# TensorE's order in a loop over pairs of experts: from a scheduler's to one written in the source, staggered over three pairs

## The chip, the cores and the metric

The kernel runs on one core of one Trainium2 chip. The metric is the device time of one execution in microseconds (us). A core has five engines that run side by side, each through its own list of instructions in order: TensorE (PE in the profile: matrix products and transposes), VectorE (DVE), ScalarE (ACT), GpSimd (POOL) and SyncE (SP, which here issues the loads of weights). PE writes its results into PSUM banks, and DVE and ACT empty them.

## What is computed

A transformer of two layers, 512 tokens by 1024 features, all float32. Layer 0 mixes tokens by differential attention, layer 1 by compressed and selected sparse attention; behind each stands a mixture of experts. All projections are modulated by vectors that come from a condition (adaLN). The change is in the experts alone:

```python
MOE_GROUPS = 4; MOE_EXPERTS_PER_GROUP = 8      # 32 experts
MOE_TOP_K = 2; MOE_HIDDEN = D_MODEL // 4       # two experts a token, hidden 256
...
# per token and chosen expert e:
#   h = silu(x @ w_gate[e]) * (x @ w_up[e]);  out += weight * (h @ w_down[e])
```

## The kernel before

The 32 experts are taken as 16 pairs (`NPAIR`). Each expert has 64 slots for its tokens, so a pair has 128 rows. `experts` (L892 to L914) loops over the pairs; for each it queues loads of weights (`w.fetch`, on SP), gathers the 128 token rows by an indirect DMA on POOL (`gather`, L826), and calls `pair` (L830 to L890). One pair is worked in these steps, whose letters are used from here on:

- **R**: 8 transposes of the gathered rows `xg` (L840) into two PSUM banks of the kind `b_tr`, four in each; each of the 8 results is modulated on its way to `xT`, by DVE (L847) and ACT (L845) in turn.
- **G**: the products with gate and up (L852), 16 for each of the two experts, in one bank `b_mm`. The two experts' instructions use 64 of the array's columns each and run side by side; PE counts 32 instructions. Behind them ACT makes `sl` (L855) and DVE multiplies it to `ac` (L857).
- **H**: 2 transposes of `ac` (L861) into a bank `b_tr`, copied to `aTm` by `copy_any`, which takes ACT (L382) and DVE (L383) in turn, call by call: for one pair the one, for the next the other.
- **D**: the product with down, 16 instructions (L875), 8 into a bank `b_sc` (the first 512 features, z = 0), 8 into a `b_mm` (z = 1). DVE scales each half to `y` (L878), ACT rounds it to `yh` (L358), DVE makes the rest `yl` (L359).
- **A**: the rows are added to their tokens. DVE builds a 0/1 matrix `st` (L869); for each of 4 blocks of tokens and 2 halves z, two products (L886 with `yh`, L887 with `yl`) of 128 columns give a bank, `b_sc` for z = 0, `b_mm` for z = 1, and DVE adds it to the accumulator `xs` (L888). That is 16 instructions on PE and 8 additions on DVE.

PSUM has two banks `b_tr`, two `b_sc` and four `b_mm`; a bank is written again only when its readers are through. Weights lie in buffers that are freed by their last use: a pair's 12 pieces of 512 KB are 6.29 MB.

In the source, pair q runs R, G, H, then A of pair q-1 (`between`), then D. The order that each engine gets is set by a scheduler when the program is built; it moves instructions among pairs as it sees fit. `overflow` calls `pair` too, for experts with more than 64 tokens; its branch is not taken with these inputs.

```python
aT = mp.tile([P, 2, P], F32, name="aTm", bufs=2)
copy_any(aT.rearrange("p k t -> p (k t)"), b[:, 0:HID])
if between is not None:
    between()
```

Of the kernel before, what the change touches and what calls it, by code (L numbers as in the profile page):

```python
# [11 lines left out]
F32 = mybir.dt.float32  # L12
# [69 lines left out]
def tile_kernel(ctx, tc, x, c, positions, ada_w, ada_b, norm_g, final_g, diff_w_in, diff_w_out,  # L82
# [3 lines left out]
    nc = tc.nc  # L86
    mm = nc.tensor.matmul
    x_d = x.rearrange("b s d -> (b s) d")
# [296 lines left out]
    class Experts:  # L385
# [65 lines left out]
    def x_first():  # L451
        for t in range(NT):
            nc.sync.dma_start(o_n[:, t, :], x_d[t * P:(t + 1) * P, :])
            normed(m, o_n[:, t, :], o_n[:, t, :], r0[:, t:t + 1], ("a", 2))
        for k in range(KC):
            b = bank("tr")
            for t in range(NT):
                nc.tensor.transpose(b[:, t * P:(t + 1) * P], by_k(o_n[:, t, :])[:, k, :], ident)
            copy_any(xT[k // 4][:, k % 4, :], b)
# [23 lines left out]
    def qk_unit(u, before=None):  # L483
# [34 lines left out]
    def diff_rows(h, i, qs, kh, kl, v, hc):  # L518
# [15 lines left out]
        for j in range(i + 1):  # L534
            nc.tensor.transpose(b[:, j * P:(j + 1) * P], a[:, j * P:(j + 1) * P], ident)
        aT = m.tile([P, 512], F32, name="aT", bufs=2)
# [77 lines left out]
    def o_trans(h):  # L614
        b = bank("tr")
        for i in range(NT):
            nc.tensor.transpose(b[:, i * P:(i + 1) * P], o_n[:, i, h * P:(h + 1) * P], ident)
        stack_k(b, o_hi[:, h, :], o_lo[:, h, :])
# [63 lines left out]
    def logits(g, lb, t):  # L682

        xk = by_k(g.xs[:, t, :])
        for q in range(2):
            b = bank("tr")
            for kk in range(4):
                nc.tensor.transpose(b[:, kk * P:(kk + 1) * P], xk[:, 4 * q + kk, :], ident)
            ht = g.mp.tile([P, 512], F32, name="ht", tag="xT", bufs=2)
# [139 lines left out]

    def pair(g, q, tab, gu, dn, xg, between=None):  # L830


        mp = g.mq
        toks, tokf, wts = tab
        xT = g.mp.tile([P, KC, P], F32, name="xT", bufs=2)
        for z in range(2):
            b = bank("tr")
            for kk in range(4):
                k = 4 * z + kk
                nc.tensor.transpose(b[:, kk * P:(kk + 1) * P], by_k(xg)[:, k, :], ident)  # L840
            for kk in range(4):
# [4 lines left out]
                else:  # L846
                    nc.vector.tensor_scalar(xT[:, k, :], src, g.Ac[:, k:k + 1], g.shc[:, k:k + 1],  # L847
                                            op0=OP.mult, op1=OP.add)
        hb = bank("mm")
        for k in range(KC):  # L850
            for a in range(2):
                mm(hb[64 * a:64 * a + 64, :].rearrange("p (z n) -> p z n", z=2), xT[:, k, 64 * a:64 * a + 64], gu(a, k),  # L852
                   start=(k == 0), stop=(k == KC - 1), skip_group_check=True)
        sl = mp.tile([P, HID], F32, name="sl", bufs=2)
        nc.scalar.activation(sl, hb[:, 0:HID], AF.Silu)  # L855
        ac = mp.tile([P, HID], F32, name="ac", bufs=2)
        nc.vector.tensor_tensor(ac.rearrange("p (k t) -> p t k", k=2), hb[:, HID:512].rearrange("p (t k) -> p t k", k=2),  # L857
                                sl.rearrange("p (t k) -> p t k", k=2), op=OP.mult)
        b = bank("tr")
        for k in range(2):  # L860
            nc.tensor.transpose(b[:, k * P:(k + 1) * P], ac[:, k * P:(k + 1) * P], ident)  # L861
        aT = mp.tile([P, 2, P], F32, name="aTm", bufs=2)
        copy_any(aT.rearrange("p k t -> p (k t)"), b[:, 0:HID])
        if between is not None:
            between()
        yh = mp.tile([P, D], F32R, name="yh", bufs=1)
# [13 lines left out]

        def add():
            for t in range(NT):
                for z in range(2):
                    zz = slice(z * 512, (z + 1) * 512)
                    b = bank("mm" if z else "sc")
                    mm(b, st[:, t * P:(t + 1) * P], yh[:, zz], start=True, stop=False)  # L886
                    mm(b, st[:, t * P:(t + 1) * P], yl[:, zz], start=False, stop=True)  # L887
                    nc.vector.tensor_tensor(g.xs[:, t, zz], g.xs[:, t, zz], b, op=OP.add)  # L888

        return add  # L890

    def experts(l, g, w, later):  # L892
# [11 lines left out]
        overflow(l, g, g.xg[-1])  # L904
        add = None
        for q in range(NPAIR):
            e = 2 * q
            w.fetch(q=q, paced=DEPTH_X)
            if q:
                gather(tab, q, g.xg[q % len(g.xg)])  # L910
            add = pair(g, q, tab,
                       lambda a, k: w.gu(e + a, k), lambda a, k, z: w.dn(e + a, k, z), g.xg[q % len(g.xg)], add)
        add()
        g.st2.close()  # L914

    def overflow(l, g, xg):
# [20 lines left out]
        with tc.If(cv > STEP):  # L937
            base = g.mq.tile([P, 1], F32, name="base")
            nc.vector.memset(base, 0.0)
            with tc.For_i(1, OVER, 1):  # L940
# [3 lines left out]
                for q in range(NPAIR):  # L944
                    gather(tab, q, xg)
                    pair(g, q, tab, gu(q), dn(q), xg)()

# [23 lines left out]
    def h_k(k):  # L971
        b = bank("tr")
        for t in range(NT):
            nc.tensor.transpose(b[:, t * P:(t + 1) * P], by_k(xr[t // 2][:, t % 2, :])[:, k, :], ident)
        modulate(qp, ("wh", 4), b, k, Ac, shc, hi, lo)
# [20 lines left out]
    def evac_cs(t, acc):  # L996
# [7 lines left out]
        for s in range(4):  # L1004
            nc.tensor.transpose(b[:, s * P:(s + 1) * P], tmp[:, 2 * s:2 * s + 2, :].rearrange("p a d -> p (a d)"), ident)
        bv = b.rearrange("p (s t) -> p s t", s=4)
# [6 lines left out]
        for s in range(2):  # L1013
            nc.tensor.transpose(b[:, s * P:(s + 1) * P], tmp[:, 8 + 2 * s:10 + 2 * s, :].rearrange("p a d -> p (a d)"),
                                ident)
# [3 lines left out]
    def evac_wg(t, acc):  # L1019
# [10 lines left out]
        for s in range(2):  # L1030
            nc.tensor.transpose(b[:, s * P:(s + 1) * P], tmp[:, 2 * s:2 * s + 2, :].rearrange("p a d -> p (a d)"), ident)
        for gi in range(2):
            stack_k(b[:, gi * P:(gi + 1) * P], kst["w"][gi][0][:, tt], kst["w"][gi][1][:, tt])

    def q_unit(gi):
# [6 lines left out]
        def evac(t, acc):  # L1042
# [4 lines left out]
            for half in range(2):  # L1047
                b = bank("tr")
                for s in range(4):
                    c0 = 2 * (half * 4 + s)  # L1050
                    nc.tensor.transpose(b[:, s * P:(s + 1) * P], tmp[:, c0:c0 + 2, :].rearrange("p a d -> p (a d)"),
                                        ident)
# [12 lines left out]
    b = bank("tr")  # L1065
    nc.tensor.transpose(b[:, 0:32], pos32, ident[0:32, 0:32])
    posT = m.tile([P, 32], F32, name="posT")
# [43 lines left out]
    for k in range(2):  # L1111
        nc.tensor.transpose(b[:, k * P:(k + 1) * P], hc[:, k * P:(k + 1) * P], ident)
    hcT = m.tile([P, 2, P], F32, name="hcT", tag="pcT", bufs=2)
# [24 lines left out]
    def nsa_block(gi, i):  # L1138
# [5 lines left out]
        for zi, nm in ((1, "s"), (2, "w")):  # L1144
            if nm == "w":
# [132 lines left out]
```

## Time and profile before

| | us |
|---|---|
| median of 3 runs | 1421.07 (1418.88 to 1423.15) |
| the profiled execution | 1417.2 |
| its span in the trace | 1415.4 |
| PE busy in the span | 1289.2 (91%) |
| DVE busy | 787.2 (56%) |
| ACT busy | 513.0 (36%) |
| POOL busy | 188.4 (13%) |

The span is the time from the first to the last recorded instruction; the profiled execution's own time is 1.8 us longer. The two loops over experts lie at 399 to 681 us (layer 0) and 1122.6 to 1404.4 us (layer 1). A busy time counts an instruction from its start to its end, waits left out.

### The profile page before, as it was taken

How to read it: one execution, taken by the hardware profiler on the slowest of the kernel's cores; microseconds unless marked ns; L12 is line 12 of the kernel's file. 1: busy time of each engine (PE TensorE's matmuls, PEld its weight loads, DVE VectorE, ACT ScalarE, POOL GpSimd, SP SyncE). 2: the span in 40 equal slices, each digit the busy share in tenths (PEclk: the TensorE clock that was granted, in tenths of full speed). 3: DMA queues.
4: the chain of work that ended last, by engine and by line, in shares of the span. 5: the costliest groups of instructions: out<-in, count | busy, mean ns of one | idle time of the engine just before them, and what ended most of it. 6: DMA issues, size and time to landing. Idle time of an engine off the chain costs nothing.

```text
span 1415.4 us, 18254 instructions
## 1 busy us (share of the span) xinstructions
PE 1289.2 (91%) x6431; PEld 760.4 (54%) x6431; DVE 787.2 (56%) x1791; ACT 513.0 (36%) x1188; POOL 188.4 (13%) x298
## 2 busy tenths in 40 slices
PE   4899999978879999999799799999999599999995
PEld 0687658567733544444588465556558434444342
DVE  2444756486535666655653365657635445666555
ACT  2453544454322222111453345555644222222212
POOL 0022020211110000000042211112120200000000
PEclk7999999989979999999899999999999799999998
DMA  8633673585569999992132474520063599999931
GB/s 265 218 92 129 226 236 122 185 280 194 181 240 362 389 408 407 380 346 95 52 110 90 126 251 138 139 70 1 30 183 119 167 363 376 401 409 408 363 144 60
DMA packets 104494, 309.82 MB, mean 219 GB/s; under 512 B 13776, under 2 KB 27568, under 8 KB 104388
## 3 DMA queue, kind: packets, MB, share of 16 engines
q1 hardware_dynamic: 93920, 288.59, 57.4%
q0 software_dynamic: 6240, 12.95, 2.7%
q10 hardware_dynamic: 4228, 6.96, 1.6%
q8 instruction: 55, 0.90, 0.3%
q14 instruction: 51, 0.42, 0.1%
HBM read 310.51 MB, written 6.33 MB: 224 GB/s over the span
## 4 chain that ended last, share of the span: by engine, by line
PE 65%; DVE 6%; DMA 3%; ACT 2%; issue 1%; POOL 1%; DVEq 0%; POOLq 0%; ACTq 0%
PE b_mm L852 17%; PE b_mm L1202 5%; PE b_sc L875 4%; PE b_mm L875 4%; PE b_tr L1197 3%; PE b_sc L886 2%; PE b_tr L840 2%; PE b_mm L886 2%; DVE xs L888 2%; PE b_mm L350 2%; PE b_mm L572 2%; PE b_mm L573 2%; PE b_mm L351 2%; PE b_mm L352 2%; PE b_mm L574 2%; PE b_sc L887 2%
## 5 line engine op out<-in xcount | busy, mean ns | idle before, releaser
L852 PE MATMUL b_mm<-slot,xT 128*64 128x512 f32 x640 | 200.0, 607 | 0.0
L852 PE MATMUL b_mm<-ring,xT 128*64 128x512 f32 x384 | 135.9, 597 | 0.0
L350 PE MATMUL b_mm<-wh,h_hi 128*128 128x512 f32 (+1 forms) x320 | 116.6, 394 | 8.3 <-ACT wh L346 6.6
L351 PE MATMUL b_mm<-wl,h_hi 128*128 128x512 f32 (+1 forms) x320 | 122.1, 390 | 0.0
L352 PE MATMUL b_mm<-wh,h_lo 128*128 128x512 f32 (+1 forms) x320 | 119.9, 386 | 0.0
L845 ACT ACTIVATE xT<-b_tr,col_sh,col_A 128x128 f32<-128x128 f32 x128 | 56.4, 454 | 148.2 <-DVE xT L847 146.9
L852 PEld LDWEIGHTS b_mm<-slot,xT 128*64 128x64 f32 x640 | 58.3, 139 | 87.7 <-issue 81.7
L888 DVE TENSOR_TENSOR xs<-xs,b_sc 128x512 f32<-128x512 f32 x128 | 83.1, 680 | 23.1 <-PE b_sc L887 23.1
L888 DVE TENSOR_TENSOR xs<-xs,b_mm 128x512 f32<-128x512 f32 x128 | 81.9, 679 | 19.3 <-PE b_mm L887 19.3
L826 POOL DMA_INDIRECT xg<-xr_d,toks x32 | 32.1, 1003 | 434.1 <-PE b_tr L840 417.5
L189 PE MATMUL b_mm<-ring,csil 128*32 128x512 f32 x384 | 79.2, 645 | 10.5 <-DMA ring<-in_ada_w_dram 5.6
L855 ACT ACTIVATE sl<-b_mm 128x256 f32<-128x256 f32 x32 | 12.3, 384 | 187.7 <-PE b_mm L852 187.7
L857 DVE TENSOR_TENSOR ac<-b_mm,sl 128x256 f32<-128x256 f32 x32 | 19.8, 618 | 108.4 <-ACT sl L855 108.4
L347 DVE TENSOR_TENSOR wl<-ring,wh 128x512 fp32r<-128x512 f32 (+1 forms) x80 | 53.6, 679 | 38.3 <-ACT wh L346 37.6
L374 DVE TENSOR_REDUCE nm<-b_sc 128x1 f32<-128x128 f32 (+3 forms) x116 | 54.4, 482 | 32.2 <-PE b_sc L369 31.2
L350 PEld LDWEIGHTS b_mm<-wh,h_hi 128*128 128x128 f32 x320 | 60.5, 192 | 20.1 <-ACT wh L346 7.5
L1199 ACT ACTIVATE pT<-b_tr 128x512 f32<-128x512 f32 x80 | 47.3, 597 | 62.6 <-PE b_tr L1197 62.2
L358 ACT ACTIVATE yh<-y 128x512 fp32r<-128x512 f32 x64 | 39.9, 632 | 79.4 <-DVE y L878 79.4
L352 PEld LDWEIGHTS b_mm<-wh,h_lo 128*128 128x128 f32 x320 | 60.7, 190 | 11.0
L351 PEld LDWEIGHTS b_mm<-wl,h_hi 128*128 128x128 f32 x320 | 60.6, 190 | 10.9
L852 PEld LDWEIGHTS b_mm<-ring,xT 128*64 128x64 f32 x384 | 39.9, 137 | 49.4 <-issue 46.7
L346 ACT ACTIVATE wh<-ring 128x512 fp32r<-128x512 f32 (+1 forms) x80 | 48.4, 614 | 46.3 <-PE b_mm L352 38.0
(327 smaller groups left out, 2683.5 us busy)
## 6 DMA issues: line engine op xcount, KB each, us to landing
ring<-in_ada_w_dram SPq DMA_DIRECT2D x96, 512.0 KB
slot<-in_moe_w_gate_dram SPq DMA_DIRECT2D x80, 512.0 KB
slot<-in_moe_w_up_dram SPq DMA_DIRECT2D x80, 512.0 KB
dn<-in_moe_w_down_dram SPq DMA_DIRECT2D x80, 512.0 KB
slot<-in_moe_w_down_dram SPq DMA_DIRECT2D x48, 512.0 KB
ring<-in_moe_w_gate_dram SPq DMA_DIRECT2D x48, 512.0 KB
ring<-in_moe_w_up_dram SPq DMA_DIRECT2D x48, 512.0 KB
ring<-in_diff_w_in_dram SPq DMA_DIRECT2D x24, 512.0 KB
```

The source lines that it names most:

```text
L189: mm(acc[32 * g:32 * g + 32, :], lhsT, w[:, c0:c0 + 512], start=(k == 0), stop=(k == KC - 1), skip_group_check=True)
L347: nc.vector.tensor_tensor(wl[:, :n], w[:, k, :], wh[:, :n].bitcast(F32), op=OP.subtract)
L350: mm(accs[t][:, :n], hi[:, k, tt], wh[:, :n], start=(k == 0), stop=False)
L351: mm(accs[t][:, :n], hi[:, k, tt], wl[:, :n], start=False, stop=False)
L352: mm(accs[t][:, :n], lo[:, k, tt], wh[:, :n], start=False, stop=(k == KC - 1))
L374: nc.vector.tensor_reduce(nm, b[:, :n], axis=AX.X, op=OP.max, negate=True)
L845: nc.scalar.activation(xT[:, k, :], src, AF.Identity, scale=g.Ac[:, k:k + 1], bias=g.shc[:, k:k + 1])
L852: mm(hb[64 * a:64 * a + 64, :].rearrange("p (z n) -> p z n", z=2), xT[:, k, 64 * a:64 * a + 64], gu(a, k), start=(k == 0), stop=(k == KC - ...
L875: mm(yb[64 * a:64 * a + 64, :], aT[:, k, 64 * a:64 * a + 64], dn(a, k, z), start=(k == 0), stop=(k == 1), skip_group_check=True)
L886: mm(b, st[:, t * P:(t + 1) * P], yh[:, zz], start=True, stop=False)
L888: nc.vector.tensor_tensor(g.xs[:, t, zz], g.xs[:, t, zz], b, op=OP.add)
L1202: mm(ob[64 * st:64 * st + 64, :], vst[nm][:, j, 64 * gi:64 * gi + 64], pTs[st], start=(nm == "s" and j == 0), stop=False, skip_group_check ...
```

## The change

`mm` and `transpose` become helpers that, while the name "PE" is in a set, tell the scheduler to keep the instruction where the source has it. The set holds "PE" from the first to the last instruction of the loop over pairs, and nowhere else. `pair` is split into `rows_in` (R), `gate_up` (G), `by_hidden` (H) and `down` (D, which hands back its 8 additions), and the loop works on three pairs at a time: G of pair q+1, with additions of pair q-1 in it by twos (four products each) behind k = 1, 3, 5 and 7, H of pair q, R of pair q+2, D of pair q. A wider limit for the loads goes with it.

```diff
+    def pin(i, engine):
+        return tc.keep_in_program_order(i) if engine in pinned else i
+    def mm(*a, **k):
+        return pin(nc.tensor.matmul(*a, **k), "PE")
...
-                if e >= 2 * q + (N_GU if kind == "g" else N_DN):
+                if e >= (2 * q + N_GU if kind == "g" else 2 * max(q - 1, 0) + N_DN):
...
-            e = 2 * q
-            w.fetch(q=q, paced=DEPTH_X)
-            if q:
-                gather(tab, q, g.xg[q % len(g.xg)])
-            add = pair(g, q, tab,
-                       lambda a, k: w.gu(e + a, k), lambda a, k, z: w.dn(e + a, k, z), g.xg[q % len(g.xg)], add)
-        add()
+            nxt = None
+            if q + 2 < NPAIR:
+                gather(tab, q + 2, g.xg[q % 2])
+            w.fetch(q=q + 1, paced=DEPTH_X)
+            if q + 1 < NPAIR:
+                nxt = gate_up(g, xT, gus(q + 1), some)
+            aT = by_hidden(g, ac)
+            while adds:
+                adds.pop(0)()
+            if q + 2 < NPAIR:
+                xT = rows_in(g, g.xg[q % 2])
+            adds = down(g, q, tab, aT, lambda a, k, z: w.dn(2 * q + a, k, z))
+            ac = nxt
+        for a in adds:
+            a()
```

Ahead of the loop stand R and G of pair 0 and R of pair 1. At the end, G of pair 15 holds the additions of pair 13; then come H and D of pair 14, H of pair 15, the additions of pair 14, D of pair 15 and its additions. Every engine has as many instructions of each kind as before, POOL in the same order; outside the two loops PE's order is the same.

On PE before, around one of the last pairs of layer 0 (`ring` and `slot` are weights of gate and up, `dn` of down):

```order
L852 MATMUL b_mm<-ring_72,xT 64x512
L852 MATMUL b_mm<-ring_73,xT 64x512
L861 MATMUL b_tr<-ident,ac 128x128 x2
L840 MATMUL b_tr<-ident,xg_3359 128x128 x4
L875 MATMUL b_sc<-dn_7732,aTm 64x512
L875 MATMUL b_sc<-dn_7735,aTm 64x512
```

H stands right behind the G whose `ac` it takes, and four transposes of the next pair stand between it and D. The same engine after the change, a steady pair of layer 0:

```order
L94 MATMUL b_mm<-slot_6425,xT 64x512
L94 MATMUL b_mm<-slot_6507,xT 64x512
L94 MATMUL b_sc<-yh,st 128x512
L94 MATMUL b_sc<-yl,st 128x512
L94 MATMUL b_mm<-yh,st 128x512
L94 MATMUL b_mm<-yl,st 128x512
L97 MATMUL b_tr<-ident,ac 128x128 x2
L97 MATMUL b_tr<-ident,xg_3358 128x128 x8
L94 MATMUL b_sc<-dn_3571,aTm 64x512
L94 MATMUL b_sc<-dn_3574,aTm 64x512
```

The last two additions stand between G and H, H takes the `ac` of the pair before G's, and all eight transposes R of a later pair stand between H and D. (All of PE's lines there are L94 or L97, the helpers.)

On DVE before, a pair in the middle of layer 0 whose `aTm` DVE copies:

```order
L878 SCALAR_TENSOR_TENSOR y<-b_sc,tw,bc 128x512
L878 SCALAR_TENSOR_TENSOR y<-b_mm,tw,bc 128x512
L359 TENSOR_TENSOR yl<-y,yh 128x512 x2
L857 TENSOR_TENSOR ac<-b_mm,sl 128x128x2
L888 TENSOR_TENSOR xs<-xs,b_sc 128x512 x2
L888 TENSOR_TENSOR xs<-xs,b_mm 128x512 x3
L383 COPY aTm<-b_tr 128x256
```

And after, a steady pair whose `aTm` DVE copies (every second one; in the others ACT has the copy, and DVE's list is the same without it):

```order
L872 TENSOR_TENSOR ac<-b_mm,sl 128x128x2
L908 TENSOR_TENSOR xs<-xs,b_sc 128x512
L908 TENSOR_TENSOR xs<-xs,b_mm 128x512
L891 TENSOR_SCALAR st<-iota_t,tv 128x512
L394 COPY aTm<-b_tr 128x256
L855 TENSOR_SCALAR xT<-b_tr,col_A_2994,col_sh_2992 128x128 x4
L900 SCALAR_TENSOR_TENSOR y<-b_sc,tw,bc 128x512
L370 TENSOR_TENSOR yl<-y,yh 128x512
L900 SCALAR_TENSOR_TENSOR y<-b_mm,tw,bc 128x512
L370 TENSOR_TENSOR yl<-y,yh 128x512
```

The copy of `aTm` stands behind `ac` of the next pair, two additions and `st`; the four `xT` of a later pair stand behind it, and then `y` and `yl`, half by half.

## Rows read from the trace of the kernel before

**Rows 1.** Windows by stage of both loops; columns in the first line

```profile
core 0: us, PE busy (x) PEld busy (x) DVE busy (x) ACT busy (x) POOL busy (x), PEclk, DMA share, GB/s
409.61:577.16 167.55, 162.78 (x741) 75.36 (x741) 100.40 (x183) 35.76 (x76) 9.90 (x10) 0.99 1.01 390
577.16:667.96 90.80, 86.11 (x371) 37.21 (x369) 51.92 (x94) 17.59 (x37) 2.97 (x3) 1.00 0.74 271
667.96:681.00 13.04, 8.49 (x34) 4.03 (x34) 8.68 (x15) 3.55 (x6) 0.04 (x1) 0.98 0.07 27
...
1133.17:1300.70 167.53, 162.76 (x740) 75.36 (x741) 100.41 (x183) 35.75 (x76) 9.88 (x10) 0.99 1.00 390
1300.70:1391.49 90.79, 86.10 (x371) 37.23 (x369) 51.93 (x94) 17.59 (x37) 2.97 (x3) 1.00 0.63 237
1391.49:1404.40 12.91, 8.49 (x34) 4.03 (x34) 8.67 (x15) 3.42 (x6) 0.00 (x0) 0.99 0.00 0
```

**Rows 2.** Chain of work, layer 0, first pairs: start, length, engine, tile, line

```profile
418.69 0.86 PE b_mm L852 x4
419.55 0.66 PE b_sc L886 x2
420.21 0.47 PE b_sc L887 x2
420.68 1.01 PE b_mm L852 x4
...
427.05 0.54 DVE ac L857
427.59 2.30 DVE xs L888 x4
429.89 0.40 DVE st L869
430.29 0.34 DVE aTm L383
```

**Rows 3.** Chain of work, a pair in the middle of layer 0

```profile
471.35 5.15 PE b_mm L852 x24
...
479.02 0.22 PE b_tr L861 x2
...
479.71 0.45 PE b_tr L840 x4
...
481.54 1.87 PE b_mm L875 x8
483.40 1.72 PE b_mm L852 x8
```

**Rows 4.** PE's instructions in time order, waits ahead of them in brackets

```profile
430.68 3.02 PE L875 MATMUL b_sc<-dn,aTm 128*64 128x512 f32 x8 [2.05 <-DVE aTm L383]
...
593.00 0.59 PE L852 MATMUL b_mm<-ring,xT 128*64 128x512 f32 x1
...
595.99 0.44 PE L861 MATMUL b_tr<-ident,ac 128*128 128x128 f32 x2 [1.11 <-DVE ac L857]
```

**Rows 5.** DVE and ACT in time order, `sl` and `aTm` of one pair

```profile
476.57 0.39 ACT L855 ACTIVATE sl<-b_mm 128x256 f32<-128x256 f32 x1 [3.07 <-PE b_mm L852]
479.28 0.38 ACT L382 ACTIVATE aTm<-b_tr 128x256 f32<-128x256 f32 x1 [2.33 <-PE b_tr L861]
```

**Rows 6.** DVE in time order, from `y` to `yl` of one pair

```profile
413.69 0.75 DVE L878 SCALAR_TENSOR_TENSOR y<-b_sc,tw,bc 128x512 f32<-128x512 f32 x1 [0.65 <-PE b_sc L875]
...
417.23 0.69 DVE L359 TENSOR_TENSOR yl<-y,yh 128x512 fp32r<-128x512 f32 x1 [0.38 <-ACT yh L358]
```

**Rows 7.** DVE in time order, the end of layer 0's loop

```profile
678.34 2.47 DVE L888 TENSOR_TENSOR xs<-xs,b_mm 128x512 f32<-128x512 f32 x4
```

**Rows 8.** Windows of ten and twenty us inside the loop, columns as in rows 1

```profile
430.00:440.00 10.00, 9.32 (x36) 3.02 (x36) 4.88 (x10) 2.98 (x6) 0.99 (x1) 0.83 0.84 299
500.00:520.00 20.00, 20.00 (x98) 9.09 (x96) 11.74 (x22) 5.22 (x12) 1.91 (x2) 1.00 1.03 407
```

More of the change, by code (lines that the diff above doesn't have):

```diff
@@ L86, in tile_kernel, with transpose @@
     nc = tc.nc
-    mm = nc.tensor.matmul
+    pinned = set()
+    def pin(i, engine):
+        return tc.keep_in_program_order(i) if engine in pinned else i
+    def mm(*a, **k):
+        return pin(nc.tensor.matmul(*a, **k), "PE")
+    def transpose(*a):
+        return pin(nc.tensor.transpose(*a), "PE")
     x_d = x.rearrange("b s d -> (b s) d")
@@ L457, in x_first @@
             for t in range(NT):
-                nc.tensor.transpose(b[:, t * P:(t + 1) * P], by_k(o_n[:, t, :])[:, k, :], ident)
+                transpose(b[:, t * P:(t + 1) * P], by_k(o_n[:, t, :])[:, k, :], ident)
             copy_any(xT[k // 4][:, k % 4, :], b)
@@ L499, in evac @@
                     c0 = 2 * (half * 4 + s)
-                    nc.tensor.transpose(b[:, s * P:(s + 1) * P], tmp[:, c0:c0 + 2, :].rearrange("p a d -> p (a d)"),
+                    transpose(b[:, s * P:(s + 1) * P], tmp[:, c0:c0 + 2, :].rearrange("p a d -> p (a d)"),
                                         ident)
@@ L534, in diff_rows @@
         for j in range(i + 1):
-            nc.tensor.transpose(b[:, j * P:(j + 1) * P], a[:, j * P:(j + 1) * P], ident)
+            transpose(b[:, j * P:(j + 1) * P], a[:, j * P:(j + 1) * P], ident)
         aT = m.tile([P, 512], F32, name="aT", bufs=2)
@@ L616, in o_trans @@
         for i in range(NT):
-            nc.tensor.transpose(b[:, i * P:(i + 1) * P], o_n[:, i, h * P:(h + 1) * P], ident)
+            transpose(b[:, i * P:(i + 1) * P], o_n[:, i, h * P:(h + 1) * P], ident)
         stack_k(b, o_hi[:, h, :], o_lo[:, h, :])
@@ L687, in logits @@
             for kk in range(4):
-                nc.tensor.transpose(b[:, kk * P:(kk + 1) * P], xk[:, 4 * q + kk, :], ident)
+                transpose(b[:, kk * P:(kk + 1) * P], xk[:, 4 * q + kk, :], ident)
             ht = g.mp.tile([P, 512], F32, name="ht", tag="xT", bufs=2)
@@ L828, in gather, with rows_in @@
                                      bounds_check=S - 1, oob_is_err=False)
-    def pair(g, q, tab, gu, dn, xg, between=None):
-        mp = g.mq
-        toks, tokf, wts = tab
+    def rows_in(g, xg):
         xT = g.mp.tile([P, KC, P], F32, name="xT", bufs=2)
@@ L839, in pair @@
                 k = 4 * z + kk
-                nc.tensor.transpose(b[:, kk * P:(kk + 1) * P], by_k(xg)[:, k, :], ident)
+                transpose(b[:, kk * P:(kk + 1) * P], by_k(xg)[:, k, :], ident)
             for kk in range(4):
@@ L848, in pair, with gate_up @@
                                             op0=OP.mult, op1=OP.add)
+        return xT
+    def gate_up(g, xT, gu, between=None):
+        mp = g.mq
         hb = bank("mm")
@@ L853, in pair @@
                    start=(k == 0), stop=(k == KC - 1), skip_group_check=True)
+            if between is not None:
+                between(k)
         sl = mp.tile([P, HID], F32, name="sl", bufs=2)
@@ L858, in pair, with by_hidden, down @@
                                 sl.rearrange("p (t k) -> p t k", k=2), op=OP.mult)
+        return ac
+    def by_hidden(g, ac):
         b = bank("tr")
         for k in range(2):
-            nc.tensor.transpose(b[:, k * P:(k + 1) * P], ac[:, k * P:(k + 1) * P], ident)
-        aT = mp.tile([P, 2, P], F32, name="aTm", bufs=2)
+            transpose(b[:, k * P:(k + 1) * P], ac[:, k * P:(k + 1) * P], ident)
+        aT = g.mq.tile([P, 2, P], F32, name="aTm", bufs=2)
         copy_any(aT.rearrange("p k t -> p (k t)"), b[:, 0:HID])
-        if between is not None:
-            between()
+        return aT
+    def down(g, q, tab, aT, dn):
+        mp = g.mq
+        toks, tokf, wts = tab
         yh = mp.tile([P, D], F32R, name="yh", bufs=1)
@@ L879, in pair, with add @@
             stack_k(y, yh[:, zz], yl[:, zz])
[L881 to L890, printed above, removed]
+        def add(t, z):
+            zz = slice(z * 512, (z + 1) * 512)
+            b = bank("mm" if z else "sc")
+            mm(b, st[:, t * P:(t + 1) * P], yh[:, zz], start=True, stop=False)
+            mm(b, st[:, t * P:(t + 1) * P], yl[:, zz], start=False, stop=True)
+            nc.vector.tensor_tensor(g.xs[:, t, zz], g.xs[:, t, zz], b, op=OP.add)
+        return [lambda t=t, z=z: add(t, z) for t in range(NT) for z in range(2)]
     def experts(l, g, w, later):
@@ L904, in experts, with gus, some @@
         overflow(l, g, g.xg[-1])
-        add = None
-        for q in range(NPAIR):
-            e = 2 * q
-            w.fetch(q=q, paced=DEPTH_X)
-            if q:
-                gather(tab, q, g.xg[q % len(g.xg)])
-            add = pair(g, q, tab,
-                       lambda a, k: w.gu(e + a, k), lambda a, k, z: w.dn(e + a, k, z), g.xg[q % len(g.xg)], add)
-        add()
+        def gus(q):
+            return lambda a, k: w.gu(2 * q + a, k)
+        gather(tab, 1, g.xg[1])
+        pinned.add("PE")
+        xT = rows_in(g, g.xg[0])
+        ac = gate_up(g, xT, gus(0))
+        xT = rows_in(g, g.xg[1])
+        adds = []
+        def some(k):
+            if k % 2:
+                for _ in range(min(2, len(adds))):
+                    adds.pop(0)()
+        for q in range(NPAIR):
+            nxt = None
[6 more added lines that the diff above has]
+            while adds:
+                adds.pop(0)()
+            if q + 2 < NPAIR:
[4 more added lines that the diff above has]
+            a()
+        pinned.clear()
         g.st2.close()
@@ L945, in overflow @@
                     gather(tab, q, xg)
-                    pair(g, q, tab, gu(q), dn(q), xg)()
+                    for a in down(g, q, tab, by_hidden(g, gate_up(g, rows_in(g, xg), gu(q))), dn(q)):
+                        a()
     g = open_moe(0)
@@ L973, in h_k @@
         for t in range(NT):
-            nc.tensor.transpose(b[:, t * P:(t + 1) * P], by_k(xr[t // 2][:, t % 2, :])[:, k, :], ident)
+            transpose(b[:, t * P:(t + 1) * P], by_k(xr[t // 2][:, t % 2, :])[:, k, :], ident)
         modulate(qp, ("wh", 4), b, k, Ac, shc, hi, lo)
@@ L1004, in evac_cs @@
         for s in range(4):
-            nc.tensor.transpose(b[:, s * P:(s + 1) * P], tmp[:, 2 * s:2 * s + 2, :].rearrange("p a d -> p (a d)"), ident)
+            transpose(b[:, s * P:(s + 1) * P], tmp[:, 2 * s:2 * s + 2, :].rearrange("p a d -> p (a d)"), ident)
         bv = b.rearrange("p (s t) -> p s t", s=4)
@@ L1013, in evac_cs @@
         for s in range(2):
-            nc.tensor.transpose(b[:, s * P:(s + 1) * P], tmp[:, 8 + 2 * s:10 + 2 * s, :].rearrange("p a d -> p (a d)"),
+            transpose(b[:, s * P:(s + 1) * P], tmp[:, 8 + 2 * s:10 + 2 * s, :].rearrange("p a d -> p (a d)"),
                                 ident)
@@ L1030, in evac_wg @@
         for s in range(2):
-            nc.tensor.transpose(b[:, s * P:(s + 1) * P], tmp[:, 2 * s:2 * s + 2, :].rearrange("p a d -> p (a d)"), ident)
+            transpose(b[:, s * P:(s + 1) * P], tmp[:, 2 * s:2 * s + 2, :].rearrange("p a d -> p (a d)"), ident)
         for gi in range(2):
@@ L1050, in evac @@
                     c0 = 2 * (half * 4 + s)
-                    nc.tensor.transpose(b[:, s * P:(s + 1) * P], tmp[:, c0:c0 + 2, :].rearrange("p a d -> p (a d)"),
+                    transpose(b[:, s * P:(s + 1) * P], tmp[:, c0:c0 + 2, :].rearrange("p a d -> p (a d)"),
                                         ident)
@@ L1065, in tile_kernel @@
     b = bank("tr")
-    nc.tensor.transpose(b[:, 0:32], pos32, ident[0:32, 0:32])
+    transpose(b[:, 0:32], pos32, ident[0:32, 0:32])
     posT = m.tile([P, 32], F32, name="posT")
@@ L1111, in tile_kernel @@
     for k in range(2):
-        nc.tensor.transpose(b[:, k * P:(k + 1) * P], hc[:, k * P:(k + 1) * P], ident)
+        transpose(b[:, k * P:(k + 1) * P], hc[:, k * P:(k + 1) * P], ident)
     hcT = m.tile([P, 2, P], F32, name="hcT", tag="pcT", bufs=2)
```

4 lines of the change are left out of this document (2 added, 2 removed).

## The prediction, made before the changed kernel had run

> **What bounds the kernel now.** I read the windows by stage first, then the chain of waits inside one pair, then PE's and DVE's instructions in time order. The windows [rows 1] show that in both loops PE is the busy engine: 162.78 of 167.55 us in the first stretch and 86.11 of 90.80 in the second; DVE has 100.40 and 51.92. From the end of the first G (409.61) to the end of the last (667.96) are 258.35 us for 15 pairs, 17.22 each; layer 1 takes 167.53 and 90.79, the same. Then come 12.9 us in which the last pair is finished, up to DVE's last addition at 678.34 + 2.47 = 680.81 [rows 7]. So the loop costs, per layer, 258.35 + 12.9 us, and PE stands still for only 4.77 + 4.69 of the former.
>
> Those waits are of two kinds [rows 4]. D waits for `aTm` (2.05 us in an early pair), because DVE has `ac`, four additions and `st` in front of the copy: 0.54, 2.30, 0.40, then 0.34 for the copy itself [rows 2]. And in the last pairs H waits 1.11 us for `ac`, since nothing stands between G and H; the rows of that kind are 5 in each layer. The first of the two has a consequence: the window behind it has a mean granted clock of 0.83 [rows 8], where the loop otherwise shows 1.00. With 2.4 GHz as 1 and 1.2 GHz as 0.5, 10 us at 0.83 are 3.4 us at the lower level, which is 1.7 us of lost work. PE had stood still for 2.05 us before. The 1.11 us waits left no such mark: their stretch has 1.00 [rows 1].
>
> The loads are not the bound: the second loop stretch asks for 271 GB/s, a full 20 us window got 407 [rows 8]. At 407 a pair's 6.29 MB take 15.5 us, less than any pair below.
>
> **What the change costs, part by part.** It adds and removes no instruction; it moves them. So I build one steady pair from the prices of the parts. A product of G or D is 5.15 / 24 = 0.215 us [rows 3]; 32 of G are 6.87, 16 of D 3.43. A product of A is 0.47 / 2 = 0.233 [rows 2]; 16 are 3.73. H is 0.22, and R, twice 0.45, is 0.90 [rows 3]. Together 15.15 us.
>
> Turns between 64-column and 128-column products have a price of their own: two products of A behind G take 0.66 where the next two take 0.47, so 0.19, say 0.20; four of G behind A take 1.01 against 0.86, so 0.15 [rows 2], and eight of D behind R 1.87 against 1.72, again 0.15 [rows 3]. The changed order has eight turns a pair: four from G to A, three from A back to G, one from R to D. D runs into the next G without one. 4 x 0.20 + 4 x 0.15 = 1.40. A pair without waits is thus 16.55 us, against 17.22 now: a gain of 0.67 a pair, if nothing waits.
>
> **Where it now waits.** H no longer waits, as its `ac` is a pair old. But between H and D stand R's eight transposes, which need both `b_tr` banks: one was free, the other is H's own, and is free only when `aTm` has been copied out of it. So R's second half waits for the copy. What the copy stands behind differs from pair to pair.
>
> Where ACT copies: H lasts 0.44 [rows 4], ACT starts 0.04 later and takes 0.38 [rows 5], 0.86 from H's start. H and R's first half take 0.22 + 0.45 = 0.67 of that. The wait costs 0.2.
>
> Where DVE copies: DVE's list has in front of the copy the `ac` of the next pair, the last two additions and `st`. Counted from the end of G's last product (476.50, in front of the `sl` at 476.57): 0.07 and 0.39 for `sl` [rows 5], 0.03 to DVE, `ac` 0.54, two additions 2.30 / 2 = 1.15, `st` 0.40, copy 0.34 [rows 2]: 2.92, with hand-offs and the additions at 0.62 (2.47 / 4, rows 7) up to 3.1; I take 3.05. PE meanwhile does four of A (0.93 + 0.20), H and R's first half, 1.13 + 0.22 + 0.45 = 1.80. It stands still for about 1.25 us, and loses 0.16 more, since a product lasts 0.59 us but the next begins after 0.43, so that an idle PE gives up its overlap [rows 3, 4]. That is 1.4. From below, the wait would be nothing if DVE came to the copy by 1.46; nothing in its order gives that. From above it is the 2.05 us row, where four additions stood in front.
>
> Behind D stands `y`, `yh`, `yl`, `y`, `yh`, `yl` in a chain over DVE and ACT: 413.69 to 417.92, 4.23 us [rows 6]. It starts when D's first half is through and the second `yl` is wanted when D's second half, eight of G, a turn and two of A are through: 1.72 + 1.72 + 0.20 + 0.47 = 4.11. With hand-offs, 0.2 us of wait a pair.
>
> So a pair with the copy on ACT takes 16.55 + 0.2 + 0.2 = 16.95, one with it on DVE 16.55 + 1.4 + 0.2 = 18.15.
>
> **The sum.** From the end of G of pair 0 to that of pair 1: R 0.90, G 6.87, turns 0.35, and about 0.45 until `xT` is there, 8.6. To pair 2, with three quarters of A's additions in it: 0.22 + 1.10 + 3.58 + 6.87 + 2.80 + 1.05 and 0.2 of wait, 15.8. Then 13 pairs, 7 of them with the copy on DVE: 7 x 18.15 + 6 x 16.95 = 228.8. Together 253.2, against 258.35: 5.1 less.
>
> The end of the loop is longer. When the last G ends, before has one pair to finish, the changed kernel two: four of A (1.1), H, the copy, D of pair 14 up to 5.5; the chain to `yl`, whose second half is there at 8.1; the eight additions of pair 14 on DVE at 0.60 to about 13, while PE, paced by the banks they free, gets to D of pair 15 at 11.4 and ends it at 15.0. The chain of its `y` ends at 17.8, and seven additions later it is 22.6. Before needs 12.9: 9.7 more. G has no more work there to lay beside these chains.
>
> Per layer +4.6, for both +9.2. PE idles in this tail twice for about 2 us (until `yl` of pair 14 and of pair 15), as long as the 2.05 us after which the clock was lower; with 1.7 us lost once or twice a layer, and the one of before's second pair gone, I add 1.4 a layer, 2.8 in all. The profiled execution's 1417.2 becomes 1429. The median of the runs is 3.9 above that execution, so the median should come to 1433.
>
> A rule of the Trainium skill speaks on the turns: TensorE: Matmul & The Clock Gate (Part 2, What happens when you issue a matmul) says that weights are loaded ahead, while the running product still streams. By it the 0.15 and 0.20 would be nothing, which the rows here contradict; and TensorEngine Tiling (Array Packing), under Key Properties, says that a change of tiling mode drains the engine, with which the rows agree.
>
> **The rivals.**
> *The clock falls at each wait for DVE's copy.* The 1.25 us lie between 1.11 (no fall) and 2.05 (fall). With 1.7 us lost after each of 7 in a layer, 14 in all, 24 us more: 1457. For it: D, which follows, is what ran slowly in the 2.05 us row. Against it: the wait is far nearer to 1.11, and PE is nearly full before it.
>
> *The copies come in time* (the other side). If DVE reaches the copy within R's first half, the waits of the 7 pairs fall from 1.4 to 0.2, 8.4 a layer, and -3.8 a layer remains: 1433 - 16.8 = 1416. If R's and the chain's 0.2 vanish too (13 x 0.4 = 5.2 a layer), 1406. The point at which it decides: +4.6 and 1.4 for the clock, 6.0 over 7 pairs, so a loss at the copy of 0.55 instead of 1.4. For it: DVE is busy for 60% of the loop only. Against it: the order of its list stands, and each entry's length is in a row.
>
> *Turns cost little in the new order.* With weights loaded ahead in the longer blocks, 1.40 falls towards 0 for 13 pairs: up to 18 a layer, 1397. The rows' blocks of four speak against it.
>
> *Nothing moves.* If the tail's 9.7 were hidden by work that follows the loop, or the pair's gain were 0.4 larger, the two would cancel: 1418 to 1425. For the first there is little, since what follows needs the finished `xs`.
>
> **How the numbers follow.** The forecast (1425 to 1443, the bounds of the copy's wait and of the clock in the tail) has a chance of 0.52. The clock at each copy 0.12. Copies in time or nearly 0.17, most of it under 1417. Cheap turns 0.05. Cancelling 0.14. A measurement here tells 0.3%, 4.3 us, from no change. Faster: 0.17 + 0.05 = 0.22, less a little that stays within the bound and with a little of the cancelling case, 0.22. Same 0.13. Slower 0.52 + 0.12 and a rest, 0.65. For 8 in 10 the range must reach down into the case of the copies in time, to 1407, and up to 1449, where the clock falls in some pairs but not all.
>
> **What would show it.** In the changed kernel's trace: no wait ahead of H; a wait of 1.1 to 1.4 us inside R in every second pair, ended by DVE's `aTm`, and almost none in the others; periods of pairs in turn near 17 and 18.2; 253 us between the first and the last G's end; some 22.6 us from there to the last addition; a granted clock near 1.00 inside the loop and lower in the tail. I am wrong if the waits inside R are missing or are 2 us, if the clock in the loop's windows is below 0.95, or if the tail is not some 10 us longer. Should the loads fall behind, waits of G or D for a weight would show; before has none.

## The result, and the profile after

The changed kernel takes 1435.01 us (median of 4 runs, 1433.62 to 1437.57) against 1421.18 before (a fourth run beside the three above): 1.0109 of it, 95% interval 1.0094 to 1.0123, 13.8 us more. The profiled execution took 1435.41 us, with a span of 1433.6; against the profiled one of before these are 18.2 us more each, since that one lay 4 us below its median and this one does not.

First the windows by stage of the changed kernel: from the end of the first G to that of the last, and from there to DVE's last addition, for layer 0 and then layer 1.

```profile
core 0: us, PE busy (x) PEld busy (x) DVE busy (x) ACT busy (x) POOL busy (x), PEclk, DMA share, GB/s
410.37:665.86 255.49, 245.96 (x1074) 102.49 (x1073) 145.69 (x261) 51.14 (x110) 12.80 (x13) 1.00 0.95 352
665.86:690.05 24.19, 19.72 (x72) 10.16 (x72) 18.12 (x32) 6.74 (x12) 0.57 (x1) 0.93 0.04 16
1144.20:1399.39 255.19, 245.93 (x1074) 102.48 (x1073) 145.69 (x261) 51.16 (x110) 12.80 (x13) 1.00 0.91 340
1399.39:1423.62 24.23, 19.74 (x73) 10.19 (x72) 18.14 (x32) 6.74 (x12) 0.57 (x1) 0.93 0.00 1
```

Against [rows 1] the loop is shorter (255.49 for 258.35) and its end nearly twice as long (24.19 for 12.86): 8.5 us more in layer 0, 8.2 in layer 1. The remaining 1.5 of the 18.2 lie outside these stretches. PE is busy for less time in the first stretch than before, 245.96 against 162.78 + 86.11 = 248.89, because more work is left for the end (72 of PE's instructions there, 34 before), and it stands still for 9.5 us of the stretch.

PE in time order, over two steady pairs of layer 0 (waits in brackets; "..." marks rows left out):

```profile
435.71 0.40 PE L94 MATMUL b_mm<-yl,st 128*128 128x512 f32 x1
435.95 0.38 PE L97 MATMUL b_tr<-ident,ac 128*128 128x128 f32 x2
436.17 0.61 PE L97 MATMUL b_tr<-ident,xg 128*128 128x128 f32 x4
438.06 0.71 PE L97 MATMUL b_tr<-ident,xg 128*128 128x128 f32 x4 [1.28 <-DVE aTm L394]
...
442.18 1.89 PE L94 MATMUL b_mm<-slot,xT 128*64 128x512 f32 x8
444.00 0.50 PE L94 MATMUL b_sc<-yh,st 128*128 128x512 f32 x1
444.33 0.39 PE L94 MATMUL b_sc<-yl,st 128*128 128x512 f32 x1
444.56 0.40 PE L94 MATMUL b_mm<-yh,st 128*128 128x512 f32 x1
444.99 0.49 PE L94 MATMUL b_mm<-yl,st 128*128 128x512 f32 x1
...
454.51 1.35 PE L97 MATMUL b_tr<-ident,xg 128*128 128x128 f32 x8
...
459.27 1.89 PE L94 MATMUL b_mm<-ring,xT 128*64 128x512 f32 x8
...
477.54 1.89 PE L94 MATMUL b_mm<-slot,xT 128*64 128x512 f32 x8
```

H (435.95) waits for nothing. R is torn in two at 438.06, by 1.28 us, in the pair whose `aTm` DVE copies; in the next pair (454.51) the list shows its eight transposes in one piece of 1.35. From G to G that is 459.27 - 442.18 = 17.09 us with the copy on ACT and 477.54 - 459.27 = 18.27 with it on DVE. The start at 444.99 shows a small loss: products of A begin 0.23 us apart, this one 0.43 after the one before, as its `yl` is only just there. From A to H, where the tile keeps its 128 columns, nothing is lost: H begins 0.24 after the last product of A (435.71).

The list of PE's waits in the same stretch (410.37 to 665.86; in total, how often, the longest) shows one kind that counts (the two others come to 0.3 and 0.2 us in all):

```profile
PE b_tr L97 <- DVE aTm L394: 8.5, 7, 1.3
```

A product of A lasts 0.40 and the next begins after 0.23, so a delay of no more than about this overlap is missing from that list. The list of the weight loads (PEld), which run ahead of the products, has two such delays besides the long one, for `yl` in every pair and for ACT's copy in the pairs without the long wait:

```profile
PEld b_tr L97 <- DVE aTm L394: 9.8, 7, 1.5
PEld b_mm L94 <- DVE yl L370: 6.5, 14, 0.5
PEld b_tr L97 <- ACT aTm L393: 1.5, 7, 0.2
```

So R is torn where ACT copies too. The same piece of 1.35, asked for in narrower windows, with ACT's copy:

```profile
454.71 0.38 ACT L393 ACTIVATE aTm<-b_tr 128x256 f32<-128x256 f32 x1 [0.93 <-PE b_tr L97]
455.15 0.71 PE L97 MATMUL b_tr<-ident,xg 128*128 128x128 f32 x4
455.36 0.50 PE L97 MATMUL b_tr<-ident,xg 128*128 128x128 f32 x3
```

Four transposes take 0.45 [rows 3], so the fifth was due at 454.96; it begins at 455.15, right behind the copy's end at 455.09, and the sixth 0.21 later instead of 0.11. Together that costs 0.3 us.

Why DVE's copy is late, the chain of work tells (start, length, engine, tile, line):

```profile
435.12 0.40 ACT sl L870
...
435.53 0.63 DVE ac L872
436.16 1.11 DVE xs L908 x2
437.27 0.40 DVE st L891
437.67 0.34 DVE aTm L394
...
438.06 0.71 PE b_tr L97 x4
```

`ac`, two additions and `st` stand on DVE between the end of G (435.03) and the copy. And the end of layer 0's loop, on PE:

```profile
673.24 0.49 PE L94 MATMUL b_mm<-yh,st 128*128 128x512 f32 x1 [0.82 <-ACT yh L369]
674.11 0.67 PE L94 MATMUL b_mm<-yl,st 128*128 128x512 f32 x1 [0.37 <-DVE yl L370]
...
675.00 0.63 PE L94 MATMUL b_sc<-yl,st 128*128 128x512 f32 x1
675.43 0.63 PE L94 MATMUL b_mm<-yh,st 128*128 128x512 f32 x1
...
678.31 0.40 PE L94 MATMUL b_mm<-yh,st 128*128 128x512 f32 x1
```

After the last G the additions of pair 14 wait for `yh` and `yl`; then they start 0.43 us apart and last 0.63 where later ones last 0.40 and start 0.23 apart: the granted clock fell to 1.2 GHz here (0.51 from 674.20 to 677.50).

### The profile page after: what moved, and what is told of

It reads as the page before. It is cut to its first block, busy times and chain, and to the rows that moved or that the text cites. A ratio compares the mean times of both kernels' runs of the same rounds, so it can differ in the third digit from the quotient of the medians.

```text
span 1433.6 us, 18153 instructions
## 1 busy us (share of the span) xinstructions
PE 1307.8 (91%) x6431; PEld 754.3 (53%) x6431; DVE 792.8 (55%) x1791; ACT 512.2 (36%) x1188; POOL 189.2 (13%) x298
## 4 chain that ended last, share of the span: by engine, by line
PE 60%; DVE 6%; ACT 2%; DMA 1%; issue 1%; POOL 1%; POOLq 0%; ACTq 0%; DVEq 0%
PE b_mm L94 41%; PE b_sc L94 13%; PE b_tr L97 6%; DVE xs L908 2%; DVE y L900 1%; DVE yl L370 1%; DVE ac L872 1%; ACT yh L369 1%; DMA xr_d<-xr 1%; DMA xg<-xr_d,toks 0%; ACT sl L870 0%; DVE nm L385 0%; DVE st L891 0%; DVE aTm L394 0%; DMA b<-in_nsa_cmp_b_dram 0%
## 5 line engine op out<-in xcount | busy, mean ns | idle before, releaser
L94 PE MATMUL b_mm<-slot,xT 128*64 128x512 f32 x640 | 200.0, 609 | 0.6 <-DVE xT L855 0.6
L908 DVE TENSOR_TENSOR xs<-xs,b_sc 128x512 f32<-128x512 f32 x128 | 87.5, 684 | 99.8 <-PE b_sc L94 99.7
L94 PE MATMUL b_mm<-ring,xT 128*64 128x512 f32 x384 | 137.0, 601 | 0.0
L94 PE MATMUL b_mm<-wh,h_hi 128*128 128x512 f32 (+1 forms) x320 | 117.0, 394 | 7.4 <-ACT wh L357 5.7
L94 PE MATMUL b_mm<-wl,h_hi 128*128 128x512 f32 (+1 forms) x320 | 122.6, 392 | 0.0
L94 PE MATMUL b_mm<-wh,h_lo 128*128 128x512 f32 (+1 forms) x320 | 119.4, 385 | 0.0
L94 PEld LDWEIGHTS b_mm<-slot,xT 128*64 128x64 f32 x640 | 52.9, 138 | 79.0 <-issue 68.7
L908 DVE TENSOR_TENSOR xs<-xs,b_mm 128x512 f32<-128x512 f32 x128 | 87.2, 681 | 3.0 <-PE b_mm L94 3.0
L94 PE MATMUL b_mm<-ring,csil 128*32 128x512 f32 x384 | 78.6, 640 | 11.0 <-DMA ring<-in_ada_w_dram 6.2
L94 PE MATMUL b_sc<-slot,slot 128*128 128x128 f32 (+3 forms) x232 | 73.2, 390 | 7.4 <-DVE hc L1155 5.5
L94 PEld LDWEIGHTS b_sc<-yh,st 128*128 128x128 f32 x128 | 24.4, 191 | 93.1 <-issue 90.9
L94 PEld LDWEIGHTS b_mm<-wh,h_hi 128*128 128x128 f32 x320 | 60.3, 191 | 18.8 <-ACT wh L357 6.3
L370 DVE TENSOR_TENSOR yl<-y,yh 128x512 fp32r<-128x512 f32 x64 | 44.3, 692 | 44.1 <-ACT yh L369 43.9
L97 PE MATMUL b_tr<-ident,xg 128*128 128x128 f32 x256 | 43.2, 296 | 27.2 <-DVE aTm L394 16.9
L94 PEld LDWEIGHTS b_mm<-wh,h_lo 128*128 128x128 f32 x320 | 60.8, 190 | 11.1
```

Of the source, the lines that this page charges most:

```text
L94: return pin(nc.tensor.matmul(*a, **k), "PE")
L97: return pin(nc.tensor.transpose(*a), "PE")
L370: nc.vector.tensor_tensor(l_out, src, h_out.bitcast(F32), op=OP.subtract)
```

## The experiments

Theory: a steady pair is PE's products, plus a price for each turn between 64 and 128 columns, plus the wait for DVE's copy in every second pair, plus a little for `yl`; and what the loop gains by this order its end loses, because two pairs are left to finish behind the last G. Rivals: the wait is only handed on; turns are free; the stagger itself, or the fixing, is what costs. All experiments change the kernel after; ratios are to the kernel before, measured beside them. The table gives layer 0 of each profiled execution in the two stages of the windows above; periods are from G to G in a steady pair.

| kernel | median us | ratio, interval | first to last G | last G to last addition | period |
|---|---|---|---|---|---|
| before | 1421.18 | | 258.35 | 12.86 | 17.22 (mean) |
| after | 1435.01 | 1.0109, 1.0094 to 1.0123 | 255.49 | 24.19 | 17.09 and 18.27 |
| copy on ACT | 1418.91 | 0.9975, 0.9959 to 0.9990 | 246.96 | 22.53 | 17.09 |
| copy on DVE | 1448.74 | 1.0197, 1.0166 to 1.0227 | 262.35 | 23.81 | 18.3 |
| order left free | 1420.83 | 0.9999, 0.9984 to 1.0014 | 257.37 | 12.86 | changing |
| fours, ACT | 1393.38 | 0.9797, 0.9759 to 0.9836 | 232.31 | 23.45 | 16.12 |
| twos later, ACT | 1410.26 | 0.9922, 0.9900 to 0.9945 | 242.94 | 22.53 | 16.82 |
| eights, ACT | 1385.75 | 0.9757, 0.9718 to 0.9795 | 227.43 | 25.44 | 15.90 |
| fours, ACT, new end | 1383.56 | 0.9730, 0.9690 to 0.9771 | 238.14 | 15.20 | 16.1 |
| eights, ACT, new end | 1379.65 | 0.9704, 0.9683 to 0.9724 | 235.72 | 16.03 | 15.9 |
| the same, order free | 1416.91 | 0.9961, 0.9944 to 0.9977 | 253.00 | 12.81 | changing |

**The copy on ACT, and on DVE.** The suspected wait is taken away, and doubled:

```diff
-        copy_any(aT.rearrange("p k t -> p (k t)"), b[:, 0:HID])
+        nc.scalar.activation(aT.rearrange("p k t -> p (k t)"), b[:, 0:HID], AF.Copy)
```

> The changed kernel with every copy of aTm in the loop on ACT. If the waits for DVE's copy are what the steady pairs lose (1.2 us more in each of 7 pairs a layer than where ACT copies), 14 x 1.2 = 17 us go away: about 1418 us, all periods near 17.1 us, no wait inside R above 0.3 us. Rival: the wait is only handed on, to yl's chain or to xT, and the time stays above 1430 us.

> The changed kernel with every copy of aTm in the loop on DVE, the same cost doubled. By the wait for DVE's copy, six more steady pairs a layer lose 1.2 us each: +14.4 us, about 1449 us, all periods near 18.3 us. Rival: the clock falls when the waits come in every pair; then well above, 1465 us or more.

The first took 1418.91 us, the second, with `nc.vector.tensor_copy` in the same place, 1448.74. In the first the list of PE's waits inside the loop keeps only one of 0.3, for `xT`; in the second it has the wait of every pair (layer 0, 411.83 to 674.18):

```profile
PE b_tr L97 <- DVE aTm L881: 15.7, 13, 1.3
```

13 waits where there were 7, each of 1.2 to 1.3 us: removing seven a layer gave 16.1 us, adding six took 13.7, 1.15 us for each. The wait is not handed on. Nor did the clock fall at it: the window of that stretch has 1.00.

```profile
411.83:674.18 262.35, 245.90 (x1074) 102.49 (x1073) 148.36 (x268) 49.18 (x103) 12.88 (x13) 1.00 0.93 343
```

**The order left free.** The staggered source, without the fixing:

```diff
-        pinned.add("PE")
```

> The changed kernel's source, staggered over three pairs, but TensorE's order left to the scheduler. If the loss is in the fixed order (eight turns a pair, the copy behind two additions, the tail), the scheduler avoids it and the time is near that of before, 1415 to 1425 us. Rival: the stagger itself, which leaves two pairs to be finished behind the last G, costs it: the tail stays at 24 us a layer and the time at 1430 us or more.

1420.83 us, as before. The trace has before's end again (12.86 us). Among the pairs PE waits 7.4 us in all, 9.1 before, but for other things (409.12 to 666.49): products of A for `yh` and for a bank that DVE's addition frees, and a little for `aTm`.

```profile
PE b_sc L94 <- ACT yh L369: 3.3, 3, 1.6
PE b_sc L94 <- DVE xs L908: 3.3, 6, 0.6
PE b_tr L97 <- DVE aTm L394: 0.8, 3, 0.4
```

So the staggered source costs nothing where the scheduler sets the order, and the 13.8 us belong to the one order that was fixed. The run does not clear the stagger itself: its end has one pair behind the last G, as before's, so the scheduler has undone the stagger there. The long end comes with the stagger as it was fixed here, and what a fixed order can do about it is tried further down. The wider limit for the loads is in this run too, and costs nothing here.

**Fours, and later twos.** With the copy on ACT, the additions come in fewer blocks, or in as many blocks that begin later:

```diff
-            if k % 2:
-                for _ in range(min(2, len(adds))):
+            if k % 4 == 3:                       # fours
+                for _ in range(min(4, len(adds))):
...
+            if k in (3, 5, 6, 7):                # twos later
+                for _ in range(min(2, len(adds))):
```

> As the run with the copy on ACT, and the additions in fours behind k = 3 and 7 instead of in twos behind 1, 3, 5 and 7. If a turn costs 0.175 us, four turns fewer a pair give 0.70 x 13 pairs x 2 layers = 18 us: about 1400 us against 1418; the chain to yl has more time too, up to 0.3 us a pair, 1392 us. Rival: turns are free in long blocks, or four additions at 0.60 us behind G make DVE late for xT: no gain, 1418 us or more.

> As the run with the copy on ACT (1418.9 us, pairs of 17.10), with the twos behind k = 3, 5, 6 and 7 instead of 1, 3, 5 and 7: as many turns, but the first additions come 1.7 us later, so that yl is there. If a pair there loses 0.28 us to yl's chain and the rest to turns, pairs of 16.8 us and about 1411 us. Rival: all the gain of the fours was the turns; then 1419 us. Other rival: all of it was the chain; then pairs of 16.1 and 1394 us.

1393.38 and 1410.26 us. The fours' pair, from G to G in time order on PE:

```profile
442.17 3.60 PE L94 MATMUL b_mm<-slot,xT 128*64 128x512 f32 x16
...
458.29 1.89 PE L94 MATMUL b_mm<-ring,xT 128*64 128x512 f32 x8
```

458.29 - 442.17 = 16.12 us for a pair that took 17.09. In the run with later twos it is 16.82, and the products of A in its first block stand 0.23 to 0.24 us apart from the second on, with no late one:

```profile
438.90 3.60 PE L94 MATMUL b_mm<-slot,xT 128*64 128x512 f32 x16
442.43 0.50 PE L94 MATMUL b_sc<-yh,st 128*128 128x512 f32 x1
442.77 0.40 PE L94 MATMUL b_sc<-yl,st 128*128 128x512 f32 x1
443.01 0.39 PE L94 MATMUL b_mm<-yh,st 128*128 128x512 f32 x1
443.24 0.40 PE L94 MATMUL b_mm<-yl,st 128*128 128x512 f32 x1
...
455.72 1.46 PE L94 MATMUL b_mm<-ring,xT 128*64 128x512 f32 x6
```

The two runs part the gain: 17.09 - 16.82 = 0.27 is the wait for `yl` (no weight load in the loop with later twos waits for it any more), 16.82 - 16.12 = 0.70 are four turns, 0.175 each. Neither rival holds, that the turns were all or that the chain was.

**Eights.** All eight additions behind k = 7, two turns fewer:

```diff
+            if k == 7:
+                for _ in range(min(8, len(adds))):
```

> As the run with fours and the copy on ACT (1393.4 us, pairs of 16.12), with all eight additions behind k = 7: two turns fewer a pair, 0.35 x 13 x 2 = 9 us less, pairs of 15.8 us and 1384 us. Rival: DVE, which needs 4.8 us for eight additions that PE makes in 3.7, holds PE up by 0.5 us a pair or more: 1397 us or above.

1385.75 us, pairs of 15.90 instead of the expected 15.8: 0.22 for two turns, not 0.35. What is missing can be read in the block of A, its weight loads and DVE:

```profile
449.08 0.40 PE L94 MATMUL b_mm<-yl,st 128*128 128x512 f32 x1
449.35 0.50 PE L94 MATMUL b_sc<-yh,st 128*128 128x512 f32 x1
449.68 0.39 PE L94 MATMUL b_sc<-yl,st 128*128 128x512 f32 x1
...
449.35 0.19 PEld L94 LDWEIGHTS b_sc<-yh,st 128*128 128x128 f32 x1 [0.31 <-DVE xs L908]
...
448.61 0.68 DVE L908 TENSOR_TENSOR xs<-xs,b_sc 128x512 f32<-128x512 f32 x1
```

The thirteenth product begins 0.27 us after the twelfth and the next 0.33 after that, where 0.23 is the rule: 0.14 us in all. It opens the fourth use of a bank `b_sc`, of which there are two; its weight load waits 0.31 us for DVE's addition from the second use, which ends at 448.61 + 0.68 = 449.29. So the trace names the bank; no run gave A a third one. The rival was right that DVE begins to hold PE up, and wrong in its size. At 15.90 us a pair the loads, 15.5 at 407 GB/s by the prediction's working, are nearly the next bound; PE's list has no wait for them yet.

**A new end.** On top of fours, and then of eights: H of pair 14 ahead of the last G, the additions of pair 13 and D of pair 14 in the middle of it, half of pair 14's additions on either side of H of pair 15.

```diff
+            if q + 2 == NPAIR:
+                aT = by_hidden(g, ac)
+                def mid(k):
+                    nonlocal adds
+                    if k == 3:
+                        for a in adds:
+                            a()
+                        adds = down(g, q, tab, aT, lambda a, k, z: w.dn(2 * q + a, k, z))
+                ac = gate_up(g, xT, gus(q + 1), mid)
+                for _ in range(4):
+                    adds.pop(0)()
+                continue
```

> As the run with fours and the copy on ACT (1393.4 us), with the end rewritten: H of pair 14 ahead of the last G, the additions of pair 13 and D of pair 14 in the middle of that G, so that G's second half lies beside the chain from D to yl. If the end's loss is waiting (0.5 for the copy, 1.2 for yh and yl, some 1.7 of clock a layer), 2.5 to 3.4 us a layer come back: about 1388 us, and no clock of 1.2 GHz in layer 0's end. Rival: the end is bound by the additions on DVE and the last pair's chain, which are as long as before: 1393 us.

> The eights (1385.8 us) and the new end together. The new end gave 2.4 us in layer 0 and 3.4 in layer 1 between the first G and the last addition, and its place is apart from the steady pairs: about 1380 us. Rival: with eights the additions pile up on DVE at the end, and the two gains overlap: 1384 us or above.

1383.56 and 1379.65 us. In the windows of the run with fours, layer 0, the end from the last G and the stretch ahead of it:

```profile
649.14:664.34 15.20, 12.46 (x50) 7.06 (x50) 13.07 (x24) 5.48 (x10) 0.57 (x1) 1.00 0.07 24
411.00:649.14 238.14, 237.43 (x1095) 109.17 (x1095) 144.33 (x261) 54.69 (x120) 12.82 (x13) 1.00 0.98 378
```

The last G lies later, as it should, and PE is busy for 237.43 of the 238.14 us ahead of its end. First G to last addition is 253.34 us against 255.76 with the old end, 2.4 less, and in layer 1 253.3 against 256.7, 3.4 less, 5.8 together; the 1.0 more in layer 1 goes with a granted clock of 0.93 in the fours' end there, which had 1.00 in layer 0. The medians differ by 9.8, the two profiled executions by 8.2. Of the 2.4 that these have beyond the 5.8, 2.1 are a wait ahead of the first G of layer 1 in the run with fours that this one had not; the rest is not accounted for. Eights with the new end need 251.75 us in layer 0, 19.5 less than before's loop. Theirs is the fastest version here, though its interval overlaps with that of fours with the new end.

**The same source, order free.** The fixing taken out of the last version:

> The same source as eights with the new end, TensorE's order left to the scheduler. If the scheduler sets the order whatever the source says, it makes its own many small blocks and turns again and the time is that of the first run with a free order, about 1418 us. Rival: a source with long blocks leads the scheduler to them: 1385 to 1395 us.

1416.91 us, 37 us more than with the order fixed. 253.00 and 12.81 us stand in place of 235.72 and 16.03. The scheduler makes its own blocks here too. Counted in the traces between the first and the last G of layer 0, PE goes from 64 to 128 columns or back 79 times before, 114 times after the change, 75 times with the first free source, 34 times with eights and the new end, and 61 times with this same source left free; and PE's list has waits here for `yh` (3.3 us) and for DVE's additions (3.5 us), of which the fixed order's list has none between these G.

## Why the prediction was right, and where its sum was off

The forecast of 1433 (1407 to 1449) holds 1435.01, and its mechanism stands: a loop that gains little because of the copy and the turns, and an end that loses more. Its sum fell short, and the median came close in part by luck.

- **The waits.** It put 1.25 us of standing in R in every second pair, 0.2 in the others, and none ahead of H. Measured: 1.2 to 1.3, seven times a layer; 0.3, which the list of PE's waits hides; and none. PE's list has no wait for a weight.
- **A steady pair** was to take 16.95 and 18.15 us; it took 17.09 and 18.27. The 0.13 in 13 pairs are 1.7 us a layer of the 2.1 by which the loop gained less than forecast (2.86 and 3.13 for 5.1). About half of that is the term for `yl`, put at 0.2 and measured at 0.27 by the later twos; the rest, where ACT copies, is the wait in R, put at 0.2 and read as 0.3. The step from G of pair 1 to that of pair 2 took 16.1, not 15.8, another 0.3.
- **The turns** at 0.15 and 0.20 were confirmed on the chip by removing four: 0.70 a pair. With 114 turns a layer for the 79 of before, the fixed order pays for 35 more, some 6 us at 0.175 each (an estimate). The rule of the Trainium skill that weights are loaded ahead (TensorE: Matmul & The Clock Gate, Part 2) does not make them free here; what it says about draining at a change of tiling mode (TensorEngine Tiling (Array Packing), Key Properties) agrees with the 0.70 us.
- **The end** was to take 22.6 us, and takes 22.53 where the clock stays at 1.00 (layer 0 of the copy on ACT), 24.19 here, where it falls once: 1.7 us, the price of [rows 8]. Its working reaches 22.0 and not 22.6 (17.8 and seven additions of 0.60); what makes up for it in the trace is the second of the last eight additions, which waits 0.59 us for PE and stands in no term. It put PE's idle time at twice about 2 us; the trace has 0.82 and 0.37 ahead of the additions of pair 14 and 1.25, in three pieces, ahead of those of pair 15. And the step to 2.8 us for the clock was badly worked: it let the fall in before's second pair count a second time, though the 258.35 us against which the loop was set hold it already. With the one fall a layer that the trace shows, 1.7 instead of 1.4, the sum would have been 12.6 for the loops' 16.7.
- **The basis.** The sum was 12 us on the profiled executions, which differ by 18.2: 16.7 in the loops, 1.5 outside. The medians differ by 13.8. So the sum lacked 6 us on the executions that it was worked out for. That the forecast for the median comes as near as 2 us is luck in part: 3.9 us were added because the profiled execution of before lay that far under its median, and the one after the change lay 0.4 us above its own.
- **The rivals.** The clock did not fall at the copies' waits (1.00 in the loop, even with 13 of them in a layer). The copies did not come in time by themselves; moved to ACT they gave 1418.91 where that rival had 1416. Turns were not cheap. And nothing cancelled.

Where the expected gain of such an order went can thus be told: it is there (17.09 us a pair with ACT's copy, 17.22 on average before), but small because of eight turns a pair, and was outweighed by the copy behind DVE's additions (1.2 us in half of the pairs) and by an end that had nothing to lie beside (11.3 us a layer, 1.7 of it clock).

## What to carry to other kernels

A fixed order is worth as much as the order that one fixes: here the same mechanism cost 1.1% in its first form and gave 3.0% after its turns, its late copy and its end were priced from the trace and removed one by one. Count the changes of tile shape in a loop as if each were an instruction, and let work that fills gaps stand in few long blocks. Where steps of several iterations are interleaved, look up for each hand-over what stands ahead of it in the queue of the engine that does it, and write the first and last iterations separately.

## What the hardware showed that was not expected

The clock did not answer to the length of a wait alone. Waits of 1.28 us in 13 pairs a layer left the granted clock at 1.00 over 262 us, and so did one of 1.6 us in the run with a free order, whose stretch has no fall. Yet the same products in the same order, with the same waits of up to 0.83 us, at the loop's end kept 1.00 in layer 0 and got 0.93 in layer 1 of one execution (copy on ACT, from the end of the last G to that of the last addition). The third row is layer 1 of the run with later twos, the fourth an instruction on DVE in the second stretch:

```profile
657.79:680.32 22.53, 18.16 (x73) 9.01 (x72) 17.55 (x31) 7.13 (x13) 0.57 (x1) 1.00 0.05 17
1384.02:1408.57 24.55, 19.74 (x72) 10.15 (x72) 19.08 (x32) 7.12 (x13) 1.13 (x2) 0.93 0.04 18
...
1373.73:1397.81 24.08, 18.19 (x72) 9.02 (x72) 18.99 (x32) 7.13 (x13) 1.12 (x2) 1.00 0.05 18
...
1405.44 1.28 DVE L1299 SCALAR_TENSOR_TENSOR xs<-xs,rs,bc 128x1024 f32<-128x1024 f32 x1
```

The 2.0 us between the first two rows are not the price of the fall. In layer 1 DVE does a piece of the final normalization (1.28 us) among the last additions, and with it the same end takes 24.08 us at a clock of 1.00. What the fall costs depends on where it comes: 1.7 us ahead of D of the last pair (24.19 against 22.53), 0.5 among the last additions, where DVE's own work hides part of it. With eights and the new end it came in both layers' ends (0.89), with fours and the new end in neither (1.00). What decides it between two such stretches stays open.
